# Operand tiles at other addresses within 128 bytes

## The chip, the cores and the metric

The kernel runs on one core of one Trainium2 chip. The metric is device time in microseconds (us) of one launch. A granted clock of 1.00 in the profile is TensorE's upper level of 2.4 GHz; the lower level is 1.2 GHz.

## What is computed

The reference is two transformer blocks on 512 tokens of width 1024, all in float32. Cut to its order:

```
h = concat(meta (16 tokens), x)                       # block 1, 528 tokens
h = h + 0.5 * swiglu(rmsnorm(h), w1, w3, w2)          # FFN 1, width 2816
q, k, v, u, g_attn, g_ssm = split(rmsnorm(h) @ w_in)
h = h + (sigmoid(g_attn) * window_attention(q, k, v)
         + sigmoid(g_ssm) * glu(gelu(s5(u)))) @ w_out
h = h + 0.5 * swiglu(rmsnorm(h), ...)                 # FFN 2
x = rmsnorm(h)[16:]                                   # block 2, 512 tokens
for layer in (MLA, GLA):                              # two kinds of attention
    x = layer_norm(a * x + mixer(x))
    x = layer_norm(a * x + conv_ffn(x))               # width 2 x 2816, causal conv of 3
    x = x + sigmoid(x @ w_gate + b) * (p @ w_proj)    # per-layer embedding
```

## The kernel before

**Layout.** Activations lie feature-major: a tile is 128 features on the partitions by 528 tokens (block 1) or 512 tokens (from FFN 2 on, which no longer needs the 16 meta tokens). A width of 1024 is eight such tiles.

**Products.** A float32 product is made of three products of float32r operands. Each operand is split into a rounded part and a rest: weights into `whi` and `wlo` (`fetch`), activations into `zh`, `zl` (`split_scaled`, `split`, `Norm.apply`), gated middles of an FFN into `mh`, `ml`, and likewise `yh/yl`, `gh/gl`, `oqh/oql`, `ovh/ovl`, `pth/ptl`. `mm3` (line 173 issues) walks the contraction by tiles of 128 and issues, for each, hi x hi, lo x hi, hi x lo: the weights are the stationary operand (128x128), the activation tile is the moving operand. Every matmul loads its stationary operand anew. `nat` (line 189) makes token-major products: there a slice of the activation tile is stationary and 256 columns of the weights move.

**Columns.** `C528 = ((0, 264), (264, 528))`: the 528 tokens of block 1 go as two matmuls of 264 columns, into the two banks of a PSUM tile `mm` of `[P, 2, 512]`; `v2` and `v` view other operands as two halves to match. `C512 = ((16, 528),)`: query and gate products of block 1 take columns 16 to 528 in one matmul. `CS = ((0, 512),)`: all of FFN 2 and block 2.

**Pools and addresses.** Pools are stacked in SBUF in the order of their opening, tiles in the order of their allocation, each rounded up to 32 bytes: `cp` (with `vec`, 472 columns), `wp` (`raw`, `whi`, `wlo`, 4096 bytes each), `sm`, `zp` (`zh0, zl0, zh1, ...`, 16 tiles, then `acc`, two `sq`, `R`), then the pools of the stage. `zp` stays open to the end, so in block 2 a `zh` or `zl` still has a slot of 528 columns, 2112 bytes = 16 x 128 + 64. `whi` begins at byte 46304, `zh0` at 88224. The place of a tile within 128 bytes follows from the sizes:

```
operand (moving)                       start modulo 128, before
zh / zl, from column 0                 32 / 96
zh / zl, from column 264 (C528)        64 / 0
zh / zl, from column 16 (C512)         96 / 32
mh, ml of FFN 1 (528 wide)             buffers alternate 32, 96; from column 264: 64, 0
yh, yl, gh, gl (block 1)               32
mh, ml of FFN 2                        96
mh, ml of both conv FFNs; pth, ptl     32
oqh, oql (MLA query projection)        64
ovh, ovl (MLA key/value projection)    32
whi, wlo (stationary; moving in nat)   96
```

**Order.** A planner orders each engine's instructions by simulated times; `behind`, `chain` and `hold` pin some of them. Weights are fetched by SyncE's queue, 512 KB a chunk, five chunks ahead, split by ScalarE (`whi`) and VectorE (`wlo`).

Of the kernel before, what the change touches and what calls it, by code (L numbers as in the profile page):

```python
# [53 lines left out]
def body(nc, tc, A, out, es):  # L54
# [3 lines left out]
    zp = es.enter_context(tc.tile_pool(name="zp", bufs=1))  # L58
# [41 lines left out]
    def banks(**tags):  # L100
        """a new division of the PSUM banks"""
# [6 lines left out]
    woff = {}  # L108

# [1 line left out]
    vec = cp.tile([P, VEC.n], F32, name="vec")  # L111
# [48 lines left out]
    C528 = ((0, 264), (264, 528))  # L160
# [5 lines left out]
    def mm3(o, w, c, m0, x, cols, m=P, ks=None):  # L166
        kt = len(x)
        for k in ks or range(kt):
            a = k * c + m0
            wh, wl = w[0][:, a:a + m], w[1][:, a:a + m]  # L170
            for j, (lhs, r) in enumerate(((wh, 0), (wl, 0), (wh, 1)) if late else ((wh, 0), (wh, 1), (wl, 0))):
                for i, (c0, c1) in enumerate(cols):
                    last["pe"] = PE.matmul(o[:, i, :c1 - c0], lhs, x[k][r][:, c0:c1],  # L173
                                           start=(k == 0 and j == 0), stop=(k == kt - 1 and j == 2))

    def proj(w, c, m0, x, cols, m=P):
        o = psm() if len(cols) == 2 else pss().unsqueeze(1)
        mm3(o[:m], w, c, m0, x, cols, m)
        return o[:m]
# [25 lines left out]
        # first guess from the exponent, then a third- and a second-order step  # L205
# [19 lines left out]
    def sumsq(tiles):  # L225
        acc = zp.tile([P, T1], F32, name="acc")
        n = tiles[0].shape[1]
        for k, t in enumerate(tiles):
            if k == 0:
                act(acc[:, :n], t, AF.Square)  # L230
            else:
                sq = zp.tile([P, T1], F32, name="sq", bufs=2)
# [4 lines left out]
    def bcast(r):  # L237
        """r [token, block] -> [*, token] in PSUM"""
# [5 lines left out]
    def token_sums(acc):  # L244
        """acc [feature, token] summed over features -> [token, block] in PSUM"""
# [9 lines left out]
    def spread_rsqrt(r, R):  # L255
        """r [token, block] -> R [*, token]"""
# [8 lines left out]
    def token_rsqrt(acc, scale, eps, R=None):  # L265
        """acc -> r [token, block], R [*, token]"""
        pst = token_sums(acc)
        r = rsqrt(pst, pst.shape[1], scale, eps)
        if R is None:
            R = zp.tile([P, T1], F32, name="R")[:, :acc.shape[1]]  # L270
# [9 lines left out]
    def swiglu(ph, z, R, cols, n, w1n, w3n, w2n, hs, hook=None, early=()):  # L280
        na = len(cols)
        w = n // na
        v = lambda t: t.rearrange("p (a n) -> p a n", a=na)
        mc = tuple((c0 - cols[0][0], c1 - cols[0][0]) for c0, c1 in cols)

        def down(mids):
            seg = len(mids)
            nt = 8 // seg
            for c in range(8 // nt):
                w2 = wload(w2n, 1024)  # L290
                for mo in range(nt):
                    k = c * nt + mo
                    p2 = proj(w2, nt * P, mo * P, mids, mc)[:, :na, :w]
                    stt(v(hs[k]), p2, 0.5, v(hs[k]), ALU.mult, ALU.add)

        pend = None
        for si, seg in enumerate(SEGS):
            mids = []
            for _ in range(seg):
                p1, p3 = ((early.pop(0) if early else proj(wload(nm, 1024), P, 0, z, cols))[:, :na, :w] for nm in (w1n, w3n))  # L300
                a = ph.tile([P, n], F32, name="ta", bufs=2)
                b = ph.tile([P, n], F32, name="tb", bufs=2)
                mul(v(a), p1, v(R))
                act(a, a, AF.Silu)
                mul(v(b), p3, v(R))
# [25 lines left out]
    def horner(o, x, cs):  # L331
        """o = (((c0 * x + c1) * x + ...) * x) without the last constant"""
# [6 lines left out]
    def sincos(pool, x, sh, tag):  # L339
        """sin and cos of x: quadrant k, remainder in [-pi/4, pi/4], series"""  # L340
# [17 lines left out]
        # k mod 4 in [-2, 2]; a = cos(k pi/2), b = sin(k pi/2)  # L358
# [44 lines left out]
    def ssm_params(sp):  # L403
# [63 lines left out]
        for hf in range(2):  # L467
# [3 lines left out]
            # decay and phase over the chunks  # L471
# [16 lines left out]
            # C lambda^l and B lambda^j  # L488
# [127 lines left out]
    nc.sync.dma_start(vec[:, KD:], A["vec"][:, KD:])  # L616
# [10 lines left out]
    R = zp.tile([P, T1], F32, name="R")  # L627
# [20 lines left out]
    with tc.tile_pool(name="m1", bufs=1) as mp:  # L648
        att = mp.tile([P, 8, S], F32, name="att")
        with tc.tile_pool(name="m2", bufs=1) as ap_:  # L650
            for i4 in range(4):
                p = proj(wload("w_in", 1024), P, 0, z, C528)
                uf = ap_.tile([P, 4, MC], F32, name="uf", tag="sc", bufs=3)
                for i in range(2):
                    mul(uf[:, :, i * 66:(i + 1) * 66], p[:, i, :264].rearrange("p (m j) -> p j m", j=4),
                        R[:, i * 264:(i + 1) * 264].rearrange("p (m j) -> p j m", j=4))
                nc.sync.dma_start(u_d[i4 * P:(i4 + 1) * P], uf.rearrange("p j m -> p (j m)"))
            kw = []
            for mo in range(2):
                p = proj(wload("w_in", 1024), P, 0, z, C528)  # L660
                f = ap_.tile([P, T1], F32, name="kf", tag=f"sq{mo}")
                mul(v2(f), p[:, :, :264], v2(R))
# [27 lines left out]
            def query():  # L690
                p = proj(wload("w_in", 1024), P, 0, z, C512)
                t = (mp if len(qf) < 2 else ap_).tile([P, S], F32, name=f"q{len(qf)}")
                stt(t, p[:, 0, :], 0.125, Rr, ALU.mult, ALU.mult)
# [7 lines left out]
            def gate(t):  # L701
                mul(t, proj(wload("w_in", 1024), P, 0, z, C512)[:, 0], Rr)
# [74 lines left out]
            for ui in range(len(units) + 1):  # L777
# [6 lines left out]
                elif 5 <= ui < 8:  # L784
                    gate(zp.tile([P, T1], F32, name="acc" if ui == 5 else "sq", bufs=1 if ui == 5 else 2)[:, :S])
# [8 lines left out]
        with tc.tile_pool(name="m3", bufs=2) as gp_:  # L794
# [12 lines left out]
            for i in range(8):  # L807
# [8 lines left out]
                act(gb, qb[:, 0], AF.Tanh, scale=0.5)  # L816
                stt(gb, gb, 1.0, qa[:, 0], ALU.add, ALU.mult)
# [7 lines left out]
            for k in range(8):  # L825
                p = proj(wload("w_out", 1024), P, 0, mg, CS)
                stt(hr[k], p[:, 0], 0.5, hr[k], ALU.mult, ALU.add)
# [39 lines left out]
    class Norm:  # L867
        """Layer norm of a x + m, m arriving by tiles in PSUM; sums are taken around the mean of the first tile"""

        def __init__(self, pool, xs, a):  # L870
            self.p, self.xs, self.a = pool, xs, a
            self.aq = zp.tile([P, T1], F32, name="acc")[:, :S]
            self.ad = pool.tile([P, S], F32, name="ad", bufs=1)

        def centre(self):
            """the mean of the first tile as it stands"""
            pc = pss("s")
            PE.matmul(pc, oness, self.xs[0])
            self.c = zp.tile([P, T1], F32, name="R")[:, :S]
# [43 lines left out]
        def apply(self, g, b, li):  # L923
            """the normed tiles and their operand"""
# [37 lines left out]
    def conv_ffn(li, xs, a, mixer):  # L962
        """norm of a xs + mixer output, gated convolution FFN, norm, per-layer embedding"""
        with tc.tile_pool(name=f"cf{li}", bufs=2) as ph:
# [10 lines left out]
            def embed(w, mo):  # L975
                p = proj(w, 512, mo * P, pt, CS)[:, 0]
# [4 lines left out]
            def close(norm, name, nxt):  # L981
                """norm with independent products between its steps"""
# [17 lines left out]
            def up(j):  # L1000
                ts_ = []
                for half in range(2):
                    c = li * 132 + half * NF + j
                    late[:] = [1] * (j < 2)
                    p = proj(wload("w_up", 1024), P, 0, z, CS)[:, 0]
# [47 lines left out]
            for k in range(8):  # L1053
                late[:] = [1] * (k < 4)
                w = wload("ple_g", 1024)
                for cols in ((0, 256), (256, 512)) if li == 1 and k == 7 else CS:
                    c = slice(*cols)
                    p = proj(w, P, 0, z, (cols,))[:, 0, :c.stop - c.start]
# [16 lines left out]
    with tc.tile_pool(name="a2", bufs=2) as mp:  # L1075
        kr = mp.tile([P, S], F32, name="kr", tag="sc", bufs=4)
        mul(kr, proj(wload("mla_in", 1024), P, 0, z, CS)[:, 0], R)
        cq, ckv = [], []
        for i in range(6):
            t = mp.tile([P, S], F32, name="cq", tag="kn" if i < 2 else "qn", bufs=4)  # L1080
            mul(t, proj(wload("mla_in", 1024), P, 0, z, CS)[:, 0], R)
# [4 lines left out]
        def rotate(o, t, x):  # L1086
            """rows x1, x2 of two heads (or twice of one)"""
# [34 lines left out]
        def nope():  # L1122
            w = wload("w_uq", 1024)
            for e in range(2):
                yield proj(w, 256, e * P, oq, CS)[:, 0]

        def rope():
            yield proj(wload("w_uq", 512), P, 0, oq, CS)[:, 0]
# [20 lines left out]
        def project(pr_):  # L1149
            """queries, keys and values of two heads, a piece at a time"""  # L1150
# [24 lines left out]
        def output(gi, put=None):  # L1175
            for c in range(4):
                w = wload("mla_o", 1024)
                for mo in range(2):
                    k = c * 2 + mo
                    p = proj(w, 256, mo * P, [og[gi * 4 + i] for i in range(4)], CS)[:, 0]  # L1180
# [93 lines left out]
    with tc.tile_pool(name="g1", bufs=2) as mp:  # L1274
# [7 lines left out]
        # gate  # L1282
        p = proj(wload("gla_a", 128), 16, 0, z, CS, m=16)[:, 0]
# [272 lines left out]
```

## Time and profile before

| | |
|---|---|
| time, median of 3 runs | 2695.86 us (2693.79 to 2696.46) |
| profiled execution, first to last instruction (its only time) | 2690.5 us |
| PE matmul busy | 2644.9 us, 98% |
| DVE, ACT, POOL busy | 1588.9, 960.4, 229.6 us |
| PE's share of the chain that ended last | 94% |

How to read it: PE is TensorE's matmul side, PEld its loading of stationary operands, DVE VectorE, ACT ScalarE, POOL GpSimd. The record of a matmul is longer than its turn, since matmuls are pipelined; what one costs in a stream is the distance from its start to the next start. A piece of the chain of waits with its length and its count gives that distance as a mean.

### The profile page before, as it was taken

Reading aid. Unit: us, or ns where it says so; the run is one execution under the profiler, and the core shown is the slowest. Engines: PE = TensorE matmul, PEld = TensorE weight load, DVE = VectorE, ACT = ScalarE, POOL = GpSimd, SP = SyncE. Lnnn points to the kernel's source line nnn. Section 1 sums busy time; section 2 is a strip of 40 time slices with the busy share of each in tenths; the row PEclk is TensorE's granted clock in tenths of the full one; section 3 lists DMA queues with packets and bytes.
Section 4 is the critical chain, followed back from the end, with each engine's and each line's share of the span. In section 5 each row is a group of like instructions: output and inputs, shape, how many; then the busy total and the mean of one; then the engine's idle time right before and its main releaser. Section 6 shows DMA issues by size and latency. Waiting matters only on the chain.

```text
span 2690.5 us, 35024 instructions
## 1 busy us (share of the span) xinstructions
PE 2644.9 (98%) x13918; PEld 2189.4 (81%) x13918; DVE 1588.9 (59%) x2794; ACT 960.4 (36%) x1483; POOL 229.6 (9%) x186
## 2 busy tenths in 40 slices
PE   8999999999999999999999999999999999999999
PEld 8999999655888888887777778888877777888887
DVE  7985444685557544467665676555663456754456
ACT  4222232243333222234434344333344233433333
POOL 1000001231010000010000021000300011100030
PEclk9999999899999999999999999999999999999999
DMA  5443224332233333322111223333222222333322
GB/s 170 131 132 110 89 92 130 90 90 59 94 95 97 94 99 97 94 91 60 46 60 52 71 61 112 94 95 96 91 81 71 71 65 69 118 95 96 97 89 69
DMA packets 87748, 243.31 MB, mean 90 GB/s; under 512 B 20081, under 2 KB 26097, under 8 KB 87458
## 3 DMA queue, kind: packets, MB, share of 16 engines
q1 hardware_dynamic: 87586, 241.08, 28.9%
q8 instruction: 110, 1.80, 0.3%
q14 instruction: 52, 0.43, 0.1%
HBM read 229.11 MB, written 11.93 MB: 90 GB/s over the span
## 4 chain that ended last, share of the span: by engine, by line
PE 94%; DVE 3%; issue 1%; ACT 1%; DMA 0%; POOL 0%; SPq 0%; DVEq 0%; POOLq 0%; ACTq 0%
PE ps_b L173 62%; PE mm L173 16%; PE ps_b L189 6%; PE ps_q L1200 2%; PE ps_o L1228 1%; PE ps_q L1199 1%; PE ps_o L1365 1%; PE ps_t L1216 1%; PE ps_o L772 1%; DVE h L64 1%; PE ps_u L1354 1%; PE ps_q L719 1%; PE ps_t L756 0%; DVE sq L64 0%; DVE wlo L64 0%
## 5 line engine op out<-in xcount | busy, mean ns | idle before, releaser
L84 ACT ACTIVATE whi<-raw 128x1024 fp32r<-128x1024 f32 (+2 forms) x418 | 432.3, 1037 | 1056.6 <-PE ps_b L173 697.9
L64 DVE TENSOR_TENSOR wlo<-raw,whi 128x1024 fp32r<-128x1024 f32 (+2 forms) x418 | 518.0, 1241 | 343.8 <-ACT whi L84 341.0
L173 PE MATMUL ps_b<-zh,whi 128*128 128x512 f32 (+1 forms) x1656 | 653.5, 395 | 6.5 <-ACT zh L84 2.3
L173 PE MATMUL ps_b<-zh,wlo 128*128 128x512 f32 (+1 forms) x1656 | 654.5, 396 | 0.0
L173 PE MATMUL ps_b<-zl,whi 128*128 128x512 f32 (+1 forms) x1656 | 642.5, 391 | 0.0
L173 PEld LDWEIGHTS ps_b<-zh,whi 128*128 128x128 f32 (+1 forms) x1656 | 310.8, 188 | 82.7 <-issue 4.8
L173 PEld LDWEIGHTS ps_b<-zl,whi 128*128 128x128 f32 (+1 forms) x1656 | 311.5, 188 | 78.4 <-issue 2.6
L173 PEld LDWEIGHTS ps_b<-zh,wlo 128*128 128x128 f32 (+1 forms) x1656 | 310.8, 188 | 69.0
L173 PE MATMUL ps_b<-mh,wlo 128*128 128x512 f32 x528 | 208.5, 395 | 0.0
L173 PE MATMUL ps_b<-ml,whi 128*128 128x512 f32 x528 | 207.7, 393 | 0.0
L173 PE MATMUL ps_b<-mh,whi 128*128 128x512 f32 x528 | 207.6, 393 | 0.0
L173 PE MATMUL mm<-zh,whi 128*128 128x264 f32 x800 | 165.7, 289 | 5.8 <-ACT whi L84 5.8
L173 PE MATMUL mm<-zh,wlo 128*128 128x264 f32 x800 | 164.7, 288 | 1.7 <-DVE wlo L64 1.7
L173 PE MATMUL mm<-zl,whi 128*128 128x264 f32 x800 | 164.5, 287 | 0.7 <-DVE zl L81 0.7
L81 DVE SCALAR_TENSOR_TENSOR cv<-ps_b,vec,cv 128x511 f32<-128x511 f32 (+1 forms) x176 | 130.4, 745 | 15.9 <-ACT cv L84 14.5
L64 DVE TENSOR_TENSOR h<-h,ps_b 128x512 f32<-128x512 f32 x109 | 74.7, 686 | 106.4 <-PE ps_b L173 102.7
L173 PEld LDWEIGHTS mm<-zh,whi 128*128 128x128 f32 x800 | 126.7, 192 | 6.1 <-ACT whi L84 5.8
L173 PEld LDWEIGHTS mm<-zh,wlo 128*128 128x128 f32 x800 | 126.2, 191 | 1.9 <-DVE wlo L64 1.9
L173 PEld LDWEIGHTS mm<-zl,whi 128*128 128x128 f32 x800 | 125.5, 191 | 1.1 <-DVE zl L81 1.1
L64 POOL TENSOR_TENSOR acc<-acc,sq 128x512 f32<-128x512 f32 (+1 forms) x26 | 40.6, 1560 | 947.9 <-ACT sq L84 906.7
L173 PEld LDWEIGHTS ps_b<-mh,wlo 128*128 128x128 f32 x528 | 99.2, 188 | 23.1 <-issue 0.5
L173 PEld LDWEIGHTS ps_b<-mh,whi 128*128 128x128 f32 x528 | 99.2, 188 | 23.1 <-issue 0.5
(421 smaller groups left out, 4004.6 us busy)
## 6 DMA issues: line engine op xcount, KB each, us to landing
raw<-in_ffn_w_dram SPq DMA_DIRECT2D x130, 512.0 KB, 3.5
raw<-in_w_up_dram SPq DMA_DIRECT2D x88, 512.0 KB, 3.6
raw<-in_w_down_dram SPq DMA_DIRECT2D x44, 512.0 KB, 3.5
raw<-in_w_in_dram SPq DMA_DIRECT2D x32, 512.0 KB, 3.6
raw<-in_mla_o_dram SPq DMA_DIRECT2D x16, 512.0 KB, 3.6
raw<-in_ple_g_dram SPq DMA_DIRECT2D x16, 512.0 KB, 3.6
raw<-in_glu_dram SPq DMA_DIRECT2D x8, 512.0 KB, 3.5
raw<-in_w_out_dram SPq DMA_DIRECT2D x8, 512.0 KB, 3.4
```

The source lines that it names most:

```text
L64: return (e or V).tensor_tensor(o, a, b, op=op)
L81: return V.scalar_tensor_tensor(o, a, s, b, op0=op0, op1=op1)
L84: return SC.activation(o, a, f, **kw)
L173: last["pe"] = PE.matmul(o[:, i, :c1 - c0], lhs, x[k][r][:, c0:c1], start=(k == 0 and j == 0), stop=(k == kt - 1 and j == 2))
L189: PE.matmul(o[:m, :n], x[k][a][:, t0:t0 + m], w[b][:, kk_ * c + m0:kk_ * c + m0 + n], start=(k == 0 and i == 0), stop=(k == kt - 1 and i = ...
L719: last["sc"] = PE.matmul(pq[s_][:, :W], qf[pp * 4 + i][r, n * P:(n + 1) * P], kk)
L772: PE.matmul(po[64 * s_:64 * s_ + 64], vb[n - 1 + j][:, kv * 64:kv * 64 + 64], pT[s_][:, j], start=False, stop=(j == 1))
L1199: PE.matmul(p[:, :M_], q[rows, bs], kl[rows, :M_], start=False, stop=False)
L1200: PE.matmul(p[:, :N], d["q"][e][:, bs], d["k"][e][:, :N], start=False, stop=True)
L1216: PE.transpose(pt[:, kt * P:(kt + 1) * P], sc[:, kt * P:(kt + 1) * P], ident)
L1228: PE.matmul(po[:, b * P:(b + 1) * P], vt[:, kt, e * P:(e + 1) * P], pT[:, kt * P:(kt + 1) * P], start=(kt == 0), stop=(kt == b))
L1354: PE.matmul(pu[c][:, :256], ek[b][rows, hc], vt[hh][rows, b])
```

## The change

Tiles are put at other addresses; what is computed is the same. Comments are dropped as well. The core:

```diff
+VECS = VEC.n + 16
-    zp = es.enter_context(tc.tile_pool(name="zp", bufs=1))
+    zpc = tc.tile_pool(name="zp", bufs=1)
+    zp = zpc.__enter__()
     def psm():
-        return psp["pool"].tile([P, 2, 512], F32, tag="mm", name="mm", bufs=3)
+        t = psp["pool"].tile([P, 2, 512], F32, tag="mm", name="mm", bufs=3)
+        return t.rearrange("p a n -> p (a n)")[:, 256:256 + T1]
+    zw, aw = 544, T1
-    vec = cp.tile([P, VEC.n], F32, name="vec")
+    vec = cp.tile([P, VECS], F32, name="vec")
-    C528 = ((0, 264), (264, 528))
+    C528 = ((0, 256), (256, 528))
     def mm3(...):
-                for i, (c0, c1) in enumerate(cols):
-                    last["pe"] = PE.matmul(o[:, i, :c1 - c0], lhs, x[k][r][:, c0:c1],
+                for c0, c1 in cols:
+                    last["pe"] = PE.matmul(o[:, c0 - cols[0][0]:c1 - cols[0][0]], lhs, x[k][r][:, c0:c1],
     def split_scaled(src, g, k, n):
-        zh = zp.tile([P, n], F32R, name=f"zh{k}")
-        zl = zp.tile([P, n], F32R, name=f"zl{k}")
+        zh = zp.tile([P, zw], F32R, name=f"zh{k}")[:, :n]
+        zl = zp.tile([P, zw], F32R, name=f"zl{k}")[:, :n]
     # acc, sq, R: width T1 -> aw
     # swiglu and others: views v(...), v2(...) of two halves -> the plain 528-wide tile
-                    stt(v(hs[k]), p2, 0.5, v(hs[k]), ALU.mult, ALU.add)
+                    stt(hs[k], p2, 0.5, hs[k], ALU.mult, ALU.add)
-                for i in range(2):
-                    mul(uf[:, :, i * 66:(i + 1) * 66], ...)
+                mul(uf, p.rearrange("p (m j) -> p j m", j=4), R.rearrange("p (m j) -> p j m", j=4))
     # after w_out, ahead of the rotary tables
+    zpc.__exit__(None, None, None)
+    zpc = tc.tile_pool(name="zq", bufs=1)
+    zp = zpc.__enter__()
+    zw, aw = S, S
+    zp.tile([P, 8], F32, name="gap")
```

`vec` grows by 64 bytes, so `wp` and all that lies behind it moves by 64. In block 1 `zh` and `zl` take 544 columns, 2176 bytes = 17 x 128. Before FFN 2 the pool `zp` is closed and `zq` opened at its place; its tiles are 512 columns, 2048 bytes, behind a gap of 32 bytes. The pools stacked on it move accordingly: by 64 in block 1, by 96 (one residue lower by 32) from FFN 2 on. Added up from the sizes:

```
operand (moving)                       start modulo 128: before -> after
zh / zl in block 1, from column 0      32 / 96 -> 96 / 96
the second matmul of C528              64 / 0 (column 264) -> 96 / 96 (column 256)
zh / zl, C512                          96 / 32 -> 32 / 32
mh, ml of FFN 1, first matmul          32 or 96 -> 96 or 32
mh, ml of FFN 1, second matmul         64 or 0 -> 96 or 32
yh, yl, gh, gl                         32 -> 96
zh / zl in FFN 2 and block 2           32 / 96 -> 0 / 0
mh, ml of FFN 2                        96 -> 64
mh, ml of the conv FFNs; pth, ptl      32 -> 0
oqh, oql                               64 -> 32
ovh, ovl                               32 -> 0
whi, wlo                               96 -> 32
```

## Rows read from the trace of the kernel before

**Rows 1.** The page: busy time by engine, and the granted clock in 40 slices.
```profile
span 2690.5 us, 35024 instructions
...
PE 2644.9 (98%) x13918; PEld 2189.4 (81%) x13918; DVE 1588.9 (59%) x2794; ACT 960.4 (36%) x1483; POOL 229.6 (9%) x186
...
PEclk9999999899999999999999999999999999999999
```

**Rows 2.** The page: chain of waits, shares by engine and by line.
```profile
PE 94%; DVE 3%; issue 1%; ACT 1%; DMA 0%; POOL 0%; SPq 0%; DVEq 0%; POOLq 0%; ACTq 0%
PE ps_b L173 62%; PE mm L173 16%; PE ps_b L189 6%; PE ps_q L1200 2%; PE ps_o L1228 1%; PE ps_q L1199 1%; PE ps_o L1365 1%; PE ps_t L1216 1%; PE ps_o L772 1%; DVE h L64 1%; PE ps_u L1354 1%; PE ps_q L719 1%; PE ps_t L756 0%; DVE sq L64 0%; DVE wlo L64 0%
```

**Rows 3.** Busy time by stage: FFN 1, FFN 2, first and second conv FFN.
```profile
core 0: us, PE busy (x) PEld busy (x) DVE busy (x) ACT busy (x) POOL busy (x), PEclk, DMA share, GB/s
...
13.00:450.00 437.00, 436.85 (x3554) 434.71 (x3555) 282.48 (x593) 128.33 (x158) 16.94 (x16) 0.99 0.38 121
...
832.00:1188.00 356.00, 356.00 (x1561) 291.83 (x1559) 194.46 (x253) 106.12 (x127) 9.39 (x6) 1.00 0.31 95
...
1572.00:1958.00 386.00, 384.76 (x1658) 310.34 (x1656) 220.28 (x287) 146.39 (x186) 48.69 (x36) 0.99 0.30 92
...
2262.00:2640.00 378.00, 377.89 (x1633) 305.51 (x1632) 215.16 (x272) 143.04 (x181) 48.70 (x36) 1.00 0.31 94
```

**Rows 4.** Chain pieces (start us, us, what, count): mh of a conv FFN, of FFN 2.
```profile
1910.66 36.39 PE ps_b L173 x156
...
1135.65 43.77 PE ps_b L173 x193
```

**Rows 5.** Chain pieces: z of FFN 2, of a conv FFN; C512 query/gate; yh/yl, gh/gl.
```profile
893.70 44.15 PE ps_b L173 x192
...
1656.74 44.37 PE ps_b L173 x192
...
697.70 11.09 PE ps_b L173 x48
...
764.96 35.23 PE ps_b L173 x151
```

**Rows 6.** Chain pieces in FFN 1, 264 columns: z, then mh.
```profile
249.65 47.05 PE mm L173 x385
...
366.76 46.88 PE mm L173 x385
```

**Rows 7.** PE in order of time: first and last of 23 oq matmuls, intervals 22.
```profile
1220.53 0.40 PE L173 MATMUL ps_b<-oql,whi 128*128 128x512 f32 x1
...
1225.66 0.40 PE L173 MATMUL ps_b<-oqh,wlo 128*128 128x512 f32 x1
```

**Rows 8.** PE in order of time, 256 columns: last 48 z matmuls, first and last.
```profile
2680.22 0.28 PE L173 MATMUL ps_b<-zh,whi 128*128 128x256 f32 x1
...
2685.79 0.28 PE L173 MATMUL ps_b<-zh,wlo 128*128 128x256 f32 x1
```

**Rows 9.** The same, nat in block 2: 74 matmuls of 256 columns, first and last.
```profile
2045.06 0.28 PE L189 MATMUL ps_b<-whi,zl 128*128 128x256 f32 x1
...
2053.62 0.28 PE L189 MATMUL ps_b<-wlo,zh 128*128 128x256 f32 x1
```

**Rows 10.** Groups by line, PE (shapes, count, busy us, mean ns, idle before): counts.
```profile
L173 PE MATMUL ps_b<-zh,whi 128*128 128x512 f32 x1632 | 646.3, 396 | 6.5 <-ACT zh L84 2.3 <-DVE acc L64 1.6 <-DVE sq L64 1.2
...
L173 PE MATMUL ps_b<-mh,whi 128*128 128x512 f32 x528 | 207.6, 393 | 0.0
L173 PE MATMUL mm<-zh,whi 128*128 128x264 f32 x800 | 165.7, 289 | 5.8 <-ACT whi L84 5.8
...
L189 PE MATMUL ps_b<-whi,zh 128*128 128x256 f32 x352 | 102.6, 292 | 0.0
...
L173 PE MATMUL mm<-mh,whi 128*128 128x264 f32 x352 | 72.5, 286 | 0.0
```

More of the change, by code (lines that the diff above doesn't have):

```diff
@@ L225, in sumsq @@
     def sumsq(tiles):
-        acc = zp.tile([P, T1], F32, name="acc")
+        acc = zp.tile([P, aw], F32, name="acc")
         n = tiles[0].shape[1]
@@ L231, in sumsq @@
             else:
-                sq = zp.tile([P, T1], F32, name="sq", bufs=2)
+                sq = zp.tile([P, aw], F32, name="sq", bufs=2)
                 act(sq[:, :n], t, AF.Square)
@@ L269, in token_rsqrt @@
         if R is None:
-            R = zp.tile([P, T1], F32, name="R")[:, :acc.shape[1]]
+            R = zp.tile([P, aw], F32, name="R")[:, :acc.shape[1]]
         spread_rsqrt(r, R)
@@ L299, in swiglu @@
             for _ in range(seg):
-                p1, p3 = ((early.pop(0) if early else proj(wload(nm, 1024), P, 0, z, cols))[:, :na, :w] for nm in (w1n, w3n))
+                p1, p3 = (early.pop(0) if early else proj(wload(nm, 1024), P, 0, z, cols) for nm in (w1n, w3n))
                 a = ph.tile([P, n], F32, name="ta", bufs=2)
                 b = ph.tile([P, n], F32, name="tb", bufs=2)
-                mul(v(a), p1, v(R))
+                mul(a, p1, R)
                 act(a, a, AF.Silu)
-                mul(v(b), p3, v(R))
+                mul(b, p3, R)
                 mul(b, a, b)
@@ L615, in body @@
             part(i)
-    nc.sync.dma_start(vec[:, KD:], A["vec"][:, KD:])
+    nc.sync.dma_start(vec[:, KD:VEC.n], A["vec"][:, KD:])
     nc.sync.dma_start(ident, A["ident"])
@@ L626, in body @@
     hold["dve"] = last["rsqrt"]
-    R = zp.tile([P, T1], F32, name="R")
+    R = zp.tile([P, aw], F32, name="R")
     hold["act"] = behind(lambda: spread_rsqrt(r, R))
@@ L661, in body @@
                 f = ap_.tile([P, T1], F32, name="kf", tag=f"sq{mo}")
-                mul(v2(f), p[:, :, :264], v2(R))
+                mul(f, p, R)
                 g = ap_.tile([P, 3, 272], F32, name=f"kw{mo}")
@@ L701, in gate @@
             def gate(t):
-                mul(t, proj(wload("w_in", 1024), P, 0, z, C512)[:, 0], Rr)
+                mul(t, proj(wload("w_in", 1024), P, 0, z, C512), Rr)
                 act(t, t, AF.Tanh, scale=0.5)
@@ L784, in body @@
                 elif 5 <= ui < 8:
-                    gate(zp.tile([P, T1], F32, name="acc" if ui == 5 else "sq", bufs=1 if ui == 5 else 2)[:, :S])
+                    gate(zp.tile([P, aw], F32, name="acc" if ui == 5 else "sq", bufs=1 if ui == 5 else 2)[:, :S])
                 elif ui == 8:
@@ L815, in body @@
                 gb = gp_.tile([P, S], F32, name="gb")
-                act(gb, qb[:, 0], AF.Tanh, scale=0.5)
-                stt(gb, gb, 1.0, qa[:, 0], ALU.add, ALU.mult)
+                act(gb, qb, AF.Tanh, scale=0.5)
+                stt(gb, gb, 1.0, qa, ALU.add, ALU.mult)
                 stt(gs, gs, 1.0, gb, ALU.add, ALU.mult)
@@ L878, in centre @@
             PE.matmul(pc, oness, self.xs[0])
-            self.c = zp.tile([P, T1], F32, name="R")[:, :S]
+            self.c = zp.tile([P, aw], F32, name="R")[:, :S]
             act(self.c, pc, AF.Copy)
@@ L975, in embed @@
             def embed(w, mo):
-                p = proj(w, 512, mo * P, pt, CS)[:, 0]
+                p = proj(w, 512, mo * P, pt, CS)
                 t = ph.tile([P, S], F32, name=f"pp{len(pp)}", bufs=1)
@@ L1004, in up @@
                     late[:] = [1] * (j < 2)
-                    p = proj(wload("w_up", 1024), P, 0, z, CS)[:, 0]
+                    p = proj(wload("w_up", 1024), P, 0, z, CS)
                     late.clear()
@@ L1057, in conv_ffn @@
                     c = slice(*cols)
-                    p = proj(w, P, 0, z, (cols,))[:, 0, :c.stop - c.start]
+                    p = proj(w, P, 0, z, (cols,))
                     late.clear()
@@ L1124, in nope @@
             for e in range(2):
-                yield proj(w, 256, e * P, oq, CS)[:, 0]
+                yield proj(w, 256, e * P, oq, CS)
         def rope():
-            yield proj(wload("w_uq", 512), P, 0, oq, CS)[:, 0]
+            yield proj(wload("w_uq", 512), P, 0, oq, CS)
         def queries(d, pn, pr):
@@ L1179, in output @@
                     k = c * 2 + mo
-                    p = proj(w, 256, mo * P, [og[gi * 4 + i] for i in range(4)], CS)[:, 0]
+                    p = proj(w, 256, mo * P, [og[gi * 4 + i] for i in range(4)], CS)
                     if put:
@@ L1441, in mixer @@
         for k in range(2, 8):
-            norm.put(k, proj(wload("gla_o", 1024), P, 0, ot, CS)[:, 0])
+            norm.put(k, proj(wload("gla_o", 1024), P, 0, ot, CS))
     conv_ffn(1, hr, RT2, mixer)
     dump(hr, S)
+    zpc.__exit__(None, None, None)
     psp["cm"].__exit__(None, None, None)
```

31 lines of the change are left out of this document (12 added, 19 removed).

## The prediction

> **What bounds the kernel now.** First the page's busy times: PE is busy 98% of the span, VectorE 59%, ScalarE 36%, and the granted clock stands at 2.4 GHz nearly throughout [rows 1]. Then the chain of waits: 94% of it is PE, 62% in the products into `ps_b` and 16% in those into `mm` [rows 2]. By stage it is the same: in both kinds of FFN PE is busy 99.7 to 100% while VectorE needs 55 to 65% of the time [rows 3]. So the kernel is a stream of matmuls without holes, and a change counts by what it does to the distance between two starts. That distance I take from the chain's pieces, length over count, for stretches that hold one kind of product, and set beside it where the moving operand starts within 128 bytes (table in the description of the kernel):
>
> - `mh/ml` of a conv FFN, start 32: 36.39 / 156 = 233.3 ns; of FFN 2, start 96: 43.77 / 193 = 226.8 ns [rows 4]. Same shape, same clock, same weight slots.
> - `yh/yl`, `gh/gl`, start 32: 35.23 / 151 = 233.3 ns [rows 5]; `oqh/oql`, start 64: 5.13 us over 22 intervals = 233.2 ns [rows 7].
> - z, two matmuls at 32 and one at 96: 44.37 / 192 = 231.1 ns in a conv FFN, which is (2 x 233.3 + 226.8) / 3 = 231.1. In FFN 2, with the same z addresses, 44.15 / 192 = 230.0; for the query and gate products (two at 96, one at 32) 11.09 / 48 = 231.0, where the mean would be 229.0 [rows 5]. So the start explains most, not all.
> - 264 columns: z 47.05 / 385 = 122.2 ns, mh 46.88 / 385 = 121.8 ns [rows 6].
> - 256 columns: z (32, 96, 32) 5.57 us over 47 = 118.5 ns [rows 8]; `nat`, where the weights at 96 move, 8.56 us over 73 = 117.3 ns [rows 9]. With two of three at 32 this makes (3 x 118.5 - 117.3) / 2 = 119.1 at 32.
>
> 512 columns at 2.4 GHz are 213.3 ns, so 13.5 ns of each are lost at 96, 20 at 32 and 64. For 512 columns no operand starts at 0 now, where the change puts most of them: T(0) is the unknown.
>
> The Trainium skill ("TensorE: Matmul & The Clock Gate", section Back-to-back issue gap) gives N / 2.4 + 2.5 ns, 215.8 for 512 columns, with no word of addresses; none of the rows reaches it, and if the new address did, the sum below would be lower by another 5616 x 11.0 = 62 us, an estimate from that page.
>
> **The change part by part.** Counts are those of the groups [rows 10] and, where a group mixes stages, of the loops. Costs are matmuls x change of distance, all on the path, since PE has no holes.
>
> 1. z of FFN 2 and block 2, 32/96 to 0. The z groups hold 3 x 1632 = 4896 matmuls; 24 query and gate products x 24 = 576 of them are block 1's, so 4320 are left: 44 x 24 = 1056 in FFN 2, 3264 behind it. Bounds of T(0): from the 264-wide streams no low value shows (a second half started at 0 or 64 there and the whole costs 122, near 118.5 + 8 columns), so 233.3 stays possible; downwards 96 to 0 could bring what 64 to 96 brought, 226.8 - 6.4 = 220.4; the hard floor is 213.3. The neighbours on both sides of 0 are 96 and 32, 32 bytes off. I take the 96 row, 226.8: the distance falls as the start nears the next multiple of 128 (233.3, 233.2, 226.8), and 0 is that multiple. FFN 2: 1056 x (230.0 - 226.8) = -3.4 us. Behind it: 3264 x (231.1 - 226.8) = -14.0 us, and -0.2 for the 48 matmuls of GLA's early output.
> 2. `mh/ml` of the conv FFNs, 32 to 0: the groups have 3 x 528, two thirds are these: 1056 x (233.3 - 226.8) = -6.9 us. `pth/ptl` and `ovh/ovl`, 192 matmuls, likewise: -1.2.
> 3. `mh/ml` of FFN 2, 96 to 64: 528 x (233.2 - 226.8) = +3.4 us. This is a loss that the trace prices by itself.
> 4. `oqh/oql`, 64 to 32: 288 x 0.1 = 0.
> 5. `yh/yl/gh/gl`, 32 to 96: 8 x 24 (GLU) + 8 x 24 (w_out) = 384 x (226.8 - 233.3) = -2.5 us.
> 6. C512 products, 96/32 to 32: 576 x (233.3 - 231.0) = +1.3 us.
> 7. `nat`, moving weights 96 to 32: 3 x 352 + 192 = 1248 x (119.1 - 117.3) = +2.2 us. That the stationary operand moves as well costs nothing by the rows: in [rows 9] z is stationary at 32 and 96 in turn, and the steps stay at 0.11 to 0.12 us.
> 8. 528 columns as 256 + 272. At 96: 117.3 + 117.3 + 16 x (226.8 - 117.3) / 256 = 241.4 ns a pair, now 2 x 122.2 = 244.4: z has 3 x 800 / 2 = 1200 pairs, -3.6 us. If a partly filled line cost nothing, 272 would be 264 + 3.3 and the pair 242.8: -1.9; if the uneven pair waited for its loads as two of 272, 2 x 124.1 = 248.2: +4.6. I keep -3.6. `mh/ml` of FFN 1 (528 pairs) stay mixed: (241.4 + 119.1 + 126.2) / 2 = 243.4 against 243.5, -0.1.
> 9. VectorE reads the 528 columns as one run instead of two views; same elements, one instruction either way, four fewer for `uf`: hidden under PE, VectorE having 35% of FFN 1 free [rows 3]. Without that cover it would be 154 instructions at a few ns.
> 10. `zq` on the place of `zp`: the first write into it waits for the last reader of what lay there, the last gates; GLU and `w_out` lie between, so nothing. The float32 products of the attention stages move by 32 bytes too; they are the small PE shares of [rows 2], together some 10% of the span, and could go either way by the 2.8% between 226.8 and 233.3: 0, with +-5 us kept for the range. The planner may order anew: +-2 us.
>
> Sum: -3.4 - 14.0 - 0.2 - 6.9 - 1.2 + 3.4 - 2.5 + 1.3 + 2.2 - 3.6 - 0.1 = -25.0 us. Against the profiled execution: span 2690.5 to 2665.5. The median of the runs is 5.4 us above that span, which I leave as it is: 2695.9 - 25.0 = 2670.9 us.
>
> **The rivals.**
>
> *A. 0 is a slow start.* T(0) = 233.3 like 32 and 64. 4320 + 48 + 1056 + 192 = 5616 matmuls start there, each ns is 5.6 us: -25.0 + 5616 x 6.5 = +11.5, 2707 us, slower. It decides from T(0) = 231.3 on (25.0 / 5.616 above 226.8). For it: 0 is as near to 32 as to 96, and the halves at 0 in [rows 6] show no gain. Against it: the fall from 64 to 96 towards the boundary.
>
> *B. What counts is the distance between moving and stationary start.* Now it is 0 for FFN 2's mh (226.8), 64 for the conv FFNs' (233.3), 96 for oq (233.2). After, z and mh of block 2 stand 0 - 32 = 96 from the weights: 3264 x 2.1 + 1056 x 3.2 = +10.3; FFN 2's mh at distance 32, unknown, half of 3.4; block 1's z at 64: 1200 x (245.3 - 244.4) = +1.1; C512 and oq come to distance 0: -2.4 - 1.8. Together +8.9: 2705 us, slower. Against it: [rows 8] and [rows 9] have the same mix of distances (64, 64, 0), and differ, 118.5 and 117.3, with the moving start.
>
> *C. The address does nothing by itself.* The two z rows with equal addresses and 231.1 and 230.0 ns speak for a phase between neighbours, not a place. Then every 512-wide stream goes to about 231: 1056 x -2.2 (conv mh), 384 x -2.3, 288 x -2.2, 528 x +4.2, 1056 x +1.0 make -0.5 us, 2695 us. Against it: 233.3 and 226.8 in streams that differ in nothing but the start.
> By a rule of the Trainium skill ("SBUF — State Buffer", section Specifications (TRN2)) an access pays at each new 16-byte line; all starts here are multiples of 32, before and after, so by that rule C holds. The trace disagrees with it as it stands: 226.8 against 233.3 at starts that are all multiples of 16.
>
> **How the numbers follow.** The forecast (0 at least as good as 96) gets 0.61, A 0.15, B 0.10, C 0.14. Its own range: T(0) from 226.8, +-7 us for points 8 and 10, down to 220.4 (another -36 us): 2634 to 2678. With A and B the range goes up to 2707; I cut it at 2706 and 2636, leaving about one in ten on each side. 0.2% (5.4 us) is what a measurement can tell from no change. Faster: the forecast and 0.03 of C, 0.64. Same: the rest of C and a sliver of A and B near the break-even, 0.13. Slower: 0.23.
>
> **What would show it.** In the profile after: the distance in the conv FFNs' last down products (233.3 now) and in z (231.1 now) should both be near 226.8 or below and equal to each other; both at 233 is A or B, and then the C512 products tell them apart (A: 233, B: 227). FFN 2's mh should rise to 233; `nat` to 119; a pair in FFN 1 should take 241 ns, and PE's count stay at 13918. The prediction is wrong if z in block 2 stays at 231 or more, or if a stage loses PE's full cover.

## The result: slower by 0.6%, and the profile after

The changed kernel takes 2710.2 us (median of 4 runs, 2708.2 to 2712.5) against 2694.8 us for the kernel before beside it: a ratio of 1.0060 with a 95% interval of 1.0048 to 1.0073. The forecast of 2670.9 us was wrong in size and in sign, and 2710 lies outside its range.

The page after: span, PE's busy time and the granted clock in 40 slices, as in [rows 1], and the chain's shares by engine, as in [rows 2].

```profile
span 2708.6 us, 35030 instructions
...
PE 2663.1 (98%) x13918; PEld 2190.0 (81%) x13918; DVE 1586.8 (59%) x2790; ACT 961.0 (35%) x1483; POOL 228.9 (8%) x186
...
PEclk9999999988999999999999999999999999999999
...
PE 94%; DVE 3%; issue 1%; ACT 1%; SPq 0%; DMA 0%; POOL 0%; DVEq 0%; POOLq 0%; ACTq 0%
```

The same 13918 matmuls take 18.2 us more of PE, and the span grows by 18.1. So the reading that counted still holds: there are no new holes, the matmuls themselves take longer. The slices show one thing more: a second one has a clock under 0.9.

Busy time by stage after: FFN 1, the attention stage of block 1, FFN 2, the first conv FFN (columns as in [rows 3]).

```profile
core 0: us, PE busy (x) PEld busy (x) DVE busy (x) ACT busy (x) POOL busy (x), PEclk, DMA share, GB/s
13.00:446.00 433.00, 432.73 (x3551) 430.39 (x3551) 281.65 (x588) 128.15 (x157) 16.89 (x16) 1.00 0.39 121
485.00:669.00 184.00, 166.86 (x720) 105.28 (x718) 124.80 (x333) 67.42 (x197) 47.38 (x38) 0.89 0.24 71
839.00:1202.00 363.00, 363.00 (x1563) 292.29 (x1562) 195.46 (x254) 106.19 (x127) 9.35 (x6) 1.00 0.30 93
1587.00:1974.00 387.00, 386.32 (x1657) 310.25 (x1656) 218.94 (x285) 145.50 (x184) 48.67 (x36) 0.99 0.30 91
```

Chain pieces after (start us, length us, what, count), one stretch each: z of FFN 1, query/gate (C512), y/g, z of FFN 2, mh of FFN 2, z of a conv FFN, mh of a conv FFN. They answer to [rows 4 to 6].

```profile
246.97 46.49 PE mm L178 x384
...
703.72 11.20 PE ps_b L178 x48
...
787.93 32.20 PE ps_b L178 x138
...
901.02 44.79 PE ps_b L178 x192
...
1147.39 45.04 PE ps_b L178 x193
...
1672.28 45.03 PE ps_b L178 x193
...
1927.93 36.39 PE ps_b L178 x156
```

Length over count: every 512-wide stream but one now stands at 233.3 ns, those at start 0 (z, conv mh), at 64 (FFN 2's mh), at 32 (C512) and at 96 (y/g) alike. A pair in FFN 1 takes 242.1 ns (2 x 46.49 / 384). The exception is `oq`: 22 intervals make 5.02 us, 228.5 ns, as the first, the eleventh and the last of 23 in PE's order of time show ([rows 7] before: 233.2). Up to the eleventh an interval takes 230.0 ns, behind it 226.7.

```profile
1233.91 0.39 PE L178 MATMUL ps_b<-oql,whi 128*128 128x512 f32 x1
...
1236.21 0.39 PE L178 MATMUL ps_b<-oqh,wlo 128*128 128x512 f32 x1
...
1238.93 0.39 PE L178 MATMUL ps_b<-oqh,wlo 128*128 128x512 f32 x1
```

The span by stage, from the starts of the first products of each: FFN 1 and what follows up to the first scores -3.4 us, attention stage of block 1 +9.3 (174.8 to 184.1), the rest of block 1 +0.7, FFN 2 +6.6, MLA +1.8, first conv FFN +2.3, GLA +0.1, second conv FFN and end +0.7; together +18.1.

### The profile page after: what moved, and what is told of

Its sections match the earlier page's. It is cut to its first block, busy times and chain, and to the rows that moved or that the text cites. A ratio compares the mean times of both kernels' runs of the same rounds, so it can differ in the third digit from the quotient of the medians.

```text
span 2708.6 us, 35030 instructions
## 1 busy us (share of the span) xinstructions
PE 2663.1 (98%) x13918; PEld 2190.0 (81%) x13918; DVE 1586.8 (59%) x2790; ACT 961.0 (35%) x1483; POOL 228.9 (8%) x186
## 4 chain that ended last, share of the span: by engine, by line
PE 94%; DVE 3%; issue 1%; ACT 1%; SPq 0%; DMA 0%; POOL 0%; DVEq 0%; POOLq 0%; ACTq 0%
PE ps_b L178 62%; PE mm L178 15%; PE ps_b L194 6%; PE ps_q L1205 2%; PE ps_o L1233 1%; PE ps_q L1204 1%; PE ps_o L770 1%; PE ps_o L1370 1%; PE ps_t L1221 1%; PE ps_t L754 1%; PE ps_q L717 1%; DVE h L66 1%; PE ps_u L1359 1%; DVE wlo L66 0%; PE ps_q L1203 0%
## 5 line engine op out<-in xcount | busy, mean ns | idle before, releaser
L178 PE MATMUL ps_b<-zl,whi 128*128 128x512 f32 (+1 forms) x1656 | 649.3, 396 | 0.0
L178 PE MATMUL mm<-zh,whi 128*128 128x272 f32 (+1 forms) x800 | 163.0, 286 | 5.7 <-ACT whi L86 5.7
L178 PE MATMUL mm<-zl,whi 128*128 128x256 f32 (+1 forms) x800 | 164.1, 286 | 1.8 <-DVE zl L83 1.8
L178 PE MATMUL mm<-zh,wlo 128*128 128x272 f32 (+1 forms) x800 | 163.3, 286 | 0.6 <-DVE wlo L66 0.6
```

The lines of the kernel that those rows point to most:

```text
L178: last["pe"] = PE.matmul(o[:, c0 - cols[0][0]:c1 - cols[0][0]], lhs, x[k][r][:, c0:c1], start=(k == 0 and j == 0), stop=(k == kt - 1 and j ...
```

## Experiments

In what follows, a *stream* is a run of products of one kind without a break, and *distance* is the start of the moving operand minus the start of the stationary one, in bytes, modulo 256 (why 256 is shown by the scan below). Where a stream mixes distances, all are given. Added up from the sizes:

```
stream of 512 columns    before: distance, ns       after: distance, ns
z (zh / zl)              64,192 / 0,128  230-231    224       233.3
mh, ml of FFN 2          0               226.8      32        233.3
mh, ml of conv FFNs      192             233.3      224       233.3
yh, yl, gh, gl           192             233.3      192       233.3
oqh, oql                 224             233.2      0         228.5
C512 (zh / zl)           0,128 / 64,192  231.0      0 / 128   233.2
```

In the kernel before, every weight tile starts at 96 modulo 128, so for every 512-wide stream start and distance differ by a constant: no such row could tell one from the other. The experiments set three theories against each other. Theory R: the distance decides (rival B of the prediction). Theory X: the absolute start decides (the forecast's and rival A's ground). Theory U: 226.8 belonged to FFN 2's stage.

**e1_gap16: z and the conv FFNs' mh at distance 0.** In the changed kernel

```diff
-    zp.tile([P, 8], F32, name="gap")
+    zp.tile([P, 16], F32, name="gap")
```

> The gap of zq is 64 bytes instead of 32: z and the conv FFNs' mh/ml start where the weights start (32 modulo 128; distance 0 modulo 512), FFN 2's mh/ml at distance 64, oq at 32. Theory R (the distance between moving and stationary start decides, as rival B of the prediction has it): z and conv mh fall from 233.3 to about 226.8 ns, 5616 x 6.5 = 36.5 us, oq goes from 228.5 back to 233 (+1.3): about 2675 us. Theory X (the moving start alone decides): a start at 32 modulo 128 is slow, 233.3, and the time stays at 2710. Theory U (226.8 belonged to FFN 2's stage, not to an address): 233.3, 2710.

2682.4 us (4 runs), ratio to before 0.9958 (0.9941 to 0.9975): 32 bytes turn +0.6% into -0.4%. Theory R had 2675; the profiled execution, the shortest of the four, took 2675.6, and where the others (2681.7 to 2684.9) lost more is not shown. Chain pieces of this kernel: z of FFN 2, mh of FFN 2, z and mh of a conv FFN.

```profile
896.88 43.80 PE ps_b L178 x193
...
1137.13 44.19 PE ps_b L178 x193
...
1657.79 43.52 PE ps_b L178 x192
...
1906.16 35.65 PE ps_b L178 x157
```

226.9, 229.0, 226.7, 227.1 ns. FFN 2's mh, at distance 64 here, has a level between the two. U falls: 226.7 appears in the conv FFNs too. X had 233.3 at these starts; that another rule of starts gives these levels is what e2 tests.

**e2_both32: the same absolute starts as e1, the distances of the changed kernel.** All tiles, the weights among them, move by another 32 bytes.

```diff
-VECS = VEC.n + 16
+VECS = VEC.n + 24
```

> vec is padded by 24 columns instead of 16, the gap stays: weights and z both move by 32 bytes, z starts at the same absolute place as with the 64-byte gap (32 modulo 128), but the distance to the weights is that of the changed kernel (480 modulo 512). Theory R: z and mh stay at 233.3, time 2710. Theory X: whatever the 64-byte gap gives, this gives too.

2709.6 us (one run). z and mh of a conv FFN:

```profile
1668.40 45.03 PE ps_b L178 x193
...
1924.06 36.40 PE ps_b L178 x156
```

233.3 and 233.3 ns at the very starts that gave 226.7 in e1. X falls; R stands.

**e3_gap48 and e4_alt128: how far does the period reach?** e3 puts z and conv mh at distance 128. e4 puts zh at 0, zl at 128, and the conv FFNs' mh at 0.

```diff
 e3, in the changed kernel
-    zp.tile([P, 8], F32, name="gap")
+    zp.tile([P, 48], F32, name="gap")
 e4, in the changed kernel
-    zw, aw = S, S
-    zp.tile([P, 8], F32, name="gap")
+    zw, aw = 544, S
+    zp.tile([P, 16], F32, name="gap")
```

> The gap of zq is 192 bytes: z and conv mh at distance 128 from the weights. Theory R with a period of 128 bytes: 226.8 ns, about 2675 us. Theory R with a period of 256: 233.3, 2710. Theory X: start 32 modulo 128 as with the 64-byte gap, so the same as that one.

> A gap of 64 bytes and z tiles of 544 columns in zq: zh at distances 0 and 256, zl at 128 and 384, which is what the query and gate products of the changed kernel have, and they take 233.3. conv mh at distance 0. Theory R with a period of 128, each matmul for itself: z 226.8. With a period of 256: (2 x 226.8 + 233.3) / 3 = 229.0. If the distance only helps where all neighbours share it: 233.3 for z, 226.8 for conv mh, time about 2710 - 7 = 2703.

2706.4 and 2690.0 us (one run each). z of FFN 2 in e3; then, in e4, z of FFN 2, z and mh of a conv FFN:

```profile
898.39 44.84 PE ps_b L178 x193
```

```profile
898.05 45.03 PE ps_b L178 x193
...
1664.28 43.95 PE ps_b L178 x192
...
1914.37 35.65 PE ps_b L178 x157
```

128 is not a period: 232.3 ns in e3 (and 233.3 in z of its first conv FFN, at the same distance). In e4 the mixture 0, 0, 128 runs at 228.9 in the conv FFNs, which is (2 x 226.7 + 233.3) / 3, and at 233.3 in FFN 2, with the same addresses. The same distances, 128 alone or a mixture, can have more than one steady level.

**e5_block1, e6_block2: the two halves of the change.** e5 is the changed kernel with block 2's distances of before; e6 is the kernel before with block 2's new pool alone.

The diffs from here on are cut to their core.

```diff
 e5, in the changed kernel
-    zw, aw = S, S
-    zp.tile([P, 8], F32, name="gap")
+    zw, aw = T1, T1
 e6, in the kernel before
+    zpc.__exit__(None, None, None)
+    zpc = tc.tile_pool(name="zq", bufs=1)
+    zp = zpc.__enter__()
+    zp.tile([P, 8], F32, name="gap")
+    aw = S
 ...                                                 # widths of acc, sq, R as in the change
```

> The block 1 half of the change alone: rows of 544 and products of 256 + 272 stay, block 2's pool is a pool of its own but with rows of 528 and no gap, so that every operand of block 2 stands as far from its weights as in the kernel before, though all of it has moved by 64 bytes. Theory R (the distance between the moving and the stationary start decides): block 2 runs at the distances of before (z in FFN 2 230.0 ns, mh 226.8, z of the convolution FFNs 231.1, their mh 233.3). Theory P (the planner's new order of block 1's attention stage costs 6.5 us) adds: FFN 1 -3.8, products of 512 columns in block 1 +1.3, token-major products -1.4, attention order +6.5: +2.6 us against before, some 2697.5. Rival (the longer attention stage of the changed kernel is only its lower clock in that one execution): -3.9 us, some 2691. Rival (the absolute start decides): block 2's distances differ from before.

> The block 2 half of the change alone: block 1 is that of before, block 2 has the separate pool of 512-wide tiles with the gap of 32 bytes. Theory R: z of FFN 2 and block 2 233.3 ns (+3.5 and +7.2 us), mh of FFN 2 233.35 (+3.4), oq some 228 (-1.3): +12.8 us, some 2707.6, and block 1 as before (attention stage 176.7 us). Together with the run of the block 1 half the two must add up to the +15.3 of the whole change. Rival (the pool as such delays something, by a wait for the closing of the old one): a gap between the matmuls at the start of FFN 2, and more than +13 us.

e5 2699.6 us (11 runs), ratio 1.0019 (1.0010 to 1.0027); e6 2707.2 us (5 runs), ratio 1.0046 (1.0032 to 1.0060). Expected were 2697.5 and 2707.6. 0.19% + 0.46% = 0.65% against 0.60% for the whole: block 2 carries about 12 us, block 1 about 5. In e5, z of FFN 2, mh of FFN 2, z and mh of a conv FFN:

```profile
899.96 44.15 PE ps_b L178 x192
...
1141.91 43.54 PE ps_b L178 x192
...
1664.85 44.38 PE ps_b L178 x192
...
1918.78 36.64 PE ps_b L178 x157
```

230.0, 226.8, 231.1, 233.4 ns: the levels of [rows 4, 5], though every start has moved by 64 bytes. In e6, mh of FFN 2, 44.80 us over 192, is at 233.3. The profiled execution of e6 is the shortest of its runs, so its time is taken from the median.

**e7_zero, e9_split, e8_rows576: what the distances are worth.** e7 has the block 1 of before and every 512-wide stream from y/g on at distance 0. e9 is e7 with 256 + 272 columns in FFN 1 alone (rows of 528, attention stage as before). e8 is e7 with rows of 576 columns in block 1, which puts C512 at distance 0 throughout.

```diff
 e7, in e6
-    zp.tile([P, 8], F32, name="gap")
+    zp.tile([P, 16], F32, name="gap")
+        ph.tile([P, 112], F32, name="gap", bufs=1)      # ahead of FFN 2's tiles
+        mp.tile([P, 120], F32, name="gap", bufs=1)      # ahead of oq
+            gp_.tile([P, 80], F32, name="gap", bufs=1)  # ahead of yh
 e9, in e7
+    F528 = ((0, 256), (256, 528))                       # FFN 1 alone
 ...                                                     # and one PSUM range for both products
 e8, in e7 (the pad ahead of yh goes, the shift does its work)
+    zw = 576                                            # rows of zh, zl in block 1 (the last zl: 528)
```

> Block 1's FFN and attention of before, and in block 2 all streams of 512 columns at distance 0 from their weights: gap of 64 bytes in the pool of block 2, pads that bring FFN 2's mh, MLA's queries (oq), and the last products of block 1 (y, g) to distance 0. Theory R: all these 226.7 ns: z FFN 2 1056 x -3.3 = -3.5, other z 3264 x -4.4 = -14.4, conv mh and pth 1152 x -6.6 = -7.6, y/g 384 x -6.6 = -2.5, oq, ov, kv 400 x -6.5 = -2.6: -30.6 us, some 2664. Rival (a stream's level hangs on the neighbours, not on the distance): y/g and oq stay at 233, and the time is no better than 2669.

> The kernel with all streams at distance 0, and in FFN 1 alone the products of 256 + 272 columns over one PSUM range (rows of 528 stay, the attention stage keeps 264 + 264 and its two-part operations). If the 242 ns of a pair of 256 + 272 against 244.4 come of the split: FFN 1 shorter by 3.8 us, some 2660. If they come of the rows of 544: no gain, some 2664. Theory P in its first form (the merged products of the attention stage change what the planner puts in order there): the attention stage keeps its 176.7 us. In its second form (the planner's times at the end of FFN 1 shift the order): the stage takes some 183.

> The kernel with every stream of block 2 at distance 0, and in block 1 rows of 576 columns (2304 bytes), which puts the 576 products of 512 columns of z there at distances 0 (zh) and 256 (zl) alone, in place of 0, 64, 128, .. 448. Theory R with a period of 256 bytes: 226.7 ns instead of 231.5, 576 x -4.8 = -2.8 us against the kernel with distance 0 in block 2 alone, some 2666.5, if the order of the attention stage stays. Rival (a mixture of 0 and 256 counts as unlike): 231 to 233 ns there and no gain. The products of 264 columns change their distances too; where they feel them FFN 1 moves by more than 1 us.

- e7: 2669.3 us (4 runs), ratio 0.9902 (0.9888 to 0.9915). From the long y/g stream at the end of block 1 on, the long streams are at 226.7 to 226.9 ns, and the sum of distances was nearly earned (-26 us by the ratio, -24.5 by the medians, of the -30.6 expected). Three things took from it. The attention stage was 3.1 us longer than before in the profiled execution. `nat` in block 2 now stands at distance 0 as well, and there its 256 columns rose from a mean of 117.8 to 119.4 ns (intervals under 140 ns), some 1.8 us over 1152 products by estimate (116.9 in the changed kernel and 117.0 in e2 and e6, at 32; 119.4 in e1, e8 and e9, at 0). And y's groups of 24, which alternate with C512 products of other distances, average 228.8 ns: their first ten intervals take 224 to 236, the rest 226 to 227. `oq` begins in the same way. In e8, where C512 is at 0 too, y's groups run at 226.7 from their first product. So what ran before a stream can tell for some ten products; most streams of the scan below show no such beginning.
- e9: 2675.7 us (5 runs), ratio 0.9925 (0.9913 to 0.9937), 6.3 us worse than e7, though FFN 1 is 2.4 us shorter. The attention stage lost it (below).
- e8: 2664.7 us (4 runs), ratio 0.9884 (0.9868 to 0.9901): the best, 30 us under the kernel before. Chain pieces of e8: z of FFN 1 and C512.

```profile
246.80 46.09 PE mm L175 x384
...
707.70 11.11 PE ps_b L175 x49
```

C512 is at 226.7 ns, so 0 and 256 mixed count as alike. FFN 1's z pairs of 264 + 264 fell as well, from 244.4 to 240.1 ns, which the expectation had left open.

**e10_scan, e11_scan2: the distance by itself.** Kernels of nothing but streams of 96 products with a fresh weight load each; e10 steps the distance with 512 columns, e11 takes 256, 264 and 272 columns and pairs.

```diff
+    for d in range(0, 136, 8):
+        stream(lambda i: d)            # e10: moving start = weights' start + 4 d bytes
+    for n in (256, 264, 272):
+        for d in range(0, 64, 8):
+            stream(lambda i: d, n=n)   # e11; then pairs with the same weights
```

> Not the reference's computation: streams of 96 products alone, each with a fresh weight load, whi and wlo by turns, after one stream to start with; every stream has one distance from the weights' start to the moving start. First 0 to 512 bytes in steps of 32 with 512 columns, then fine steps, then both starts 64 bytes further, then 256 columns, then mixtures of two products at one distance and one at another. Theory R with a period of 256: 226.7 ns at 0, 256 and 512, some 229 at 64, 232 to 233 at 128 and everywhere else, the same with both starts moved. A period of 512: 226.7 at 0 and 512 alone and 233 at 256. Rival (neighbours in the program, not the distance): one level for all streams. Mixtures: the two levels weighted by their counts, or one of the two for all.

> Not the reference's computation: streams of 96 products alone, each with a fresh weight load, after one stream to start with: 256, 264 and 272 columns at distances of 0 to 224 bytes in steps of 32, then pairs on one row of operands with the same weights (256 + 272 columns, then 264 + 264) with the pair's first product at the same eight distances. Theory R for FFN 1: the gain there is by the distance as well, some 113 ns at 192 against 120 at 0 for 256 columns, pairs of 256 + 272 from 234 to 245 ns and pairs of 264 + 264 from 238 to 246, so that 240 ns for 264 + 264 at 192 and 244.4 for the distances mixed as in the kernel before are the same thing. Rival (the split as such is the gain): pairs of 256 + 272 some 2 ns under pairs of 264 + 264 at every distance, and no more than 2 ns between distances.

Chain of e10, the streams at 0, 32, 64, 96, ... 288 bytes, 96 products each:

```profile
29.62 21.76 PE stab__169 L75 x96
51.38 22.40 PE stac__267 L75 x96
73.78 21.98 PE stad__365 L75 x96
95.77 22.41 PE stae__463 L75 x96
118.18 22.40 PE staf__561 L75 x96
140.58 22.48 PE stag__659 L75 x96
163.06 22.39 PE stah__757 L75 x96
185.45 22.39 PE stai__855 L75 x96
207.84 21.77 PE staj__953 L75 x96
229.61 22.40 PE stak__1051 L75 x96
```

226.7 ns at 0 and at 256, 229.0 at 64, 233.2 to 234.2 at the others; from 256 to 512 the same again. With both starts 64 bytes further it is 226.8 at 0, 229.1 at 64 and 232.5 at 128 (233.4 without the shift). Fine steps: 233.4 at 8 bytes, 231.7 at 16, 236.3 at 240, 230.1 at 248. Mixtures: 0, 0, 256 226.8; 0, 0, 128 228.8; 0, 0, 64 231.9. So the period is 256 bytes, the good place is narrow, and there is no even slope towards it. Why the distance counts, and why 256 bytes, no run shows.

The Trainium skill ("TensorE: Matmul & The Clock Gate", section Back-to-back issue gap) gives N / 2.4 + 2.5 ns for an isolated product at the upper clock, by estimate 215.8 ns at 512 columns; no 512-wide stream reaches it here, 226.7 being the best, and the section says nothing of addresses.

Chain of e11, 256 columns at 0 and 192; then 264 + 264 at 64, 96 and 192:

```profile
30.44 11.51 PE stab__170 L76 x96
...
98.74 10.91 PE stah__758 L76 x96
...
434.59 12.00 PE stbj__3502 L103 x96
...
447.09 12.12 PE stbk__3600 L103 x96
...
484.52 11.80 PE stbn__3894 L103 x96
```

At 256 columns the order turns round: 0 is slow (119.9 ns), 192 best (113.7). The pieces of pairs hold a pause at each stream's start; over the later half, pairs of 264 + 264 go from 240.0 ns (at 0, 192, 224) to 246.8 (at 96), pairs of 256 + 272 from 239.7 (at 160) to 246.6 (at 224). Distance is worth 7 ns a pair, and the best and the worst of both splits are the same. e8's z pairs, all at 192, have just that: 240.1. At the mixed distances of before the split alone did gain (e9: z 46.38 us from first to last of 384, 242.2 ns a pair, against 244.4), which the uniform streams don't explain; over the eight distances neither split is better, and the best is reached without the new one.

**The attention stage of block 1.** Windows from the first scores to the last of them: before, e6, e8, e9, one fence each (length, PE busy, ..., PEclk).

```profile
488.00:663.00 175.00, 158.28 (x721) 102.04 (x720) 126.92 (x333) 67.43 (x197) 47.48 (x38) 0.92 0.26 75
```

```profile
487.00:660.00 173.00, 155.61 (x722) 99.91 (x720) 126.94 (x333) 67.41 (x197) 47.68 (x38) 0.94 0.27 76
```

```profile
483.00:657.00 174.00, 157.00 (x719) 101.70 (x718) 126.85 (x333) 67.08 (x197) 47.48 (x38) 0.92 0.26 75
```

```profile
486.00:672.00 186.00, 168.42 (x720) 106.01 (x718) 124.60 (x333) 67.44 (x197) 48.32 (x38) 0.88 0.25 70
```

The idle time of PE is about 17 us in each and in the stage after. What differs is the granted clock, and length times clock is nearly one number: 175 x 0.92 = 161, 173 x 0.94 = 163, 174 x 0.92 = 160, 186 x 0.88 = 164, after 184 x 0.89 = 164. So the clock makes most of the difference; some 2 us are left that it does not. In four runs with the order that PE had before (before, e6, e7, e8) the stage takes 172.6 to 177.9 us, mean 175.0; in seven where scores, values and state products lie otherwise (after, e1 to e5, e9) 181.2 to 185.7, mean 182.7. e8 starts the stage earlier than any and keeps the short time, so an early start is not it. Two stretches of 8 us after, then the same stretches before; the work in them differs with the order:

```profile
560.00:568.00 8.00, 5.10 (x27) 3.83 (x26) 7.96 (x11) 2.25 (x3) 7.52 (x5) 0.87 0.08 12
568.00:576.00 8.00, 8.00 (x23) 3.33 (x21) 3.68 (x13) 0.60 (x1) 0.00 (x0) 0.50 0.41 156
```

```profile
560.00:568.00 8.00, 7.57 (x36) 5.27 (x34) 6.93 (x15) 5.01 (x18) 3.53 (x3) 1.00 0.18 68
568.00:576.00 8.00, 5.77 (x33) 3.74 (x34) 8.00 (x14) 1.67 (x3) 5.91 (x5) 1.00 0.17 58
```

After, PE idles 2.9 us of the first stretch and runs the second at 0.50, the lower level of 1.2 GHz, 23 products in 8 us. Before, it idles 2.7 us over the two and keeps its clock. e9 against e7 shows that the split in FFN 1 alone brings the other order, in PE the very one of the changed kernel, and 8 us, with the attention stage's own operands at the same addresses. What the planner reacts to there, and whether the order alone would do it without the split, was not tried.

## Why the prediction was wrong

**The step that failed is the reading under "What bounds the kernel now" that "the start explains most", and with it point 1, "I take the 96 row, 226.8".** The start of itself explains next to nothing (e2; the scan with both starts moved differs by at most 0.9 ns, at distance 128); the distance to the weights does, and that was 0 for all products of a stream only in FFN 2's mh. The three numbers "233.3, 233.2, 226.8" were no fall towards a multiple of 128: they belong to the distances 192, 224 and 0, and the scan has 233 at the first two and 226.7 at 0 alone.

- *z and conv mh (points 1, 2)*: forecast -25.7 us with `pth`, `ovh` and GLA's early output; they came to distance 224. At 233.3 ns FFN 2's z cost +3.5 us and the rest of z +7.2 (counts times change), and conv mh changed by nothing. With 32 bytes more of a gap the forecast's levels for z and conv mh come true (e1).
- *FFN 2's mh (point 3)*: +3.4 us, right to the tenth by luck: it was forecast as start 64 and is slow as distance 32.
- *oq (point 4)*: forecast 0, measured some -0.7 us: it came to distance 0, and the 230 of its intervals that run on fell from a mean of 232.9 to 229.7 ns. *y/g (point 5)*: forecast -2.5 us, measured 0: start 96, still 192 from the weights. These two rows in the profile after already speak against the absolute start.
- *C512 (point 6)*: forecast +1.3 us, measured 576 x 2.3 = +1.3, again by luck: what came is not two starts at 32 and their like but the distances 0 and 128. *`nat` (point 7)*: forecast +2.2, measured 116.8 ns a product in the stretch of [rows 9], 1248 x -0.5 = -0.6 us.
- *The pairs of FFN 1 (point 8)*: forecast 241.4 ns and -3.6 us, measured 242.1, 1200 x -2.3 = -2.8 us (FFN 1 with what follows: -3.4): near in size. The split gave it at these distances (e9); distance alone gives more (e8).
- *The planner (point 10)*: kept at +-2 us and put at nothing in the sum. The attention stage cost +9.3 us in the profiled execution, of which the other order makes about 8 by the means above. That is the second largest term. Lower clock after a wait was in the trace of before as well and went unused: the page's slices [rows 1] show one under 0.9.

These terms add up to +20.6 us, the spans differ by +18.1. Of the rest, 1.7 us is the clock just behind the last down products, in a stretch that no term has: 0.85 over 11.2 us before, 1.00 over 9.5 us after.

Rival B had the mechanism, with a chance of 0.10, and a sum of +8.9 us. It was all but dropped for [rows 8, 9], 256-wide products with a like mix of distances and unlike times. The scan shows why these could not speak for 512 columns: at 256 the best distance is another one. Its own terms were off where it took distances modulo 128 (C512 "to distance 0" is 0 and 128, which ran at 233.2; FFN 2's mh at "half of 3.4" was the whole). Rival A forecast nearly the measured time, 2707, and its test, C512 at 233, came true; e1 and e2 show that it is false all the same: the time came out near by luck. C (the address does nothing) falls with e1.

## What to carry to other kernels

When PE is full and every matmul loads its weights anew, compare streams of one shape by the distance of the moving from the stationary start modulo 256: here 512 columns took 226.7 ns at 0, 229 at 64 and 232 to 234 at the other multiples of 32, and a `gap` tile wider by 32 bytes moved the kernel by 28 us. The best place differs with the width: what helps the 512-wide products costs `nat` with its 256. Before a row is used to choose between two explanations, look whether they are one and the same variable in it: here all weights had one residue, so for the streams that counted start and distance could not be told apart, and those rows gave no ground for 0.61 against 0.10. A change to the planner's input in one stage can reorder another that waits, as FFN 1's split did to the attention stage, and there more time at the lower clock adds to the price.

## What was not expected of the hardware

- Here the distance between two operands in SBUF, and hardly the place of either, sets the matmul's step, with a period of 256 bytes and a narrow good place at 512 columns (0: 226.7 ns; 8: 233.4; 248: 230.1).
- The best distance depends on the width: 192 for 256 columns (113.7 ns against 119.9 at 0), 0 and 192 to 224 for 264 (120.1 to 120.3 against 123.4 at 128), 160 and 192 for 272 (123.4 against 126.7).
- Several steady levels occur at the same distances: 0, 0, 128 ran at 228.8 (scan), 228.9 (e4, conv FFN) and 233.3 ns (e4, FFN 2), and 128 alone at 232.3 and 233.3 (e3). What picks the level was not found; that what ran before has a part in it, y's first ten products in e7 against those in e8 suggest.
